# A hybrid decoder layer: 32x32 block transposes on VectorE, with the blocks placed by DMA, in place of TensorE transposes

## The chip, the cores and the metric

One Trainium2 chip, one core. Five engines run their own instruction streams: TensorE (PE; its weight loads are listed as PEld), VectorE (DVE), ScalarE (ACT), GpSimd (POOL) and SyncE (SP), which here only issues DMA transfers. Waits between them go over semaphores; an engine takes its instructions in order. The metric is device time in microseconds.

## The reference

One layer, float32, 1024 tokens of width 1024. One RMS norm feeds one input projection; its columns go to two groups that mix tokens side by side, whose outputs are joined, projected, added to x and followed by an RMS norm and an MLP of width 4096.

```python
# group A: differential attention, 4 heads of two 64-wide maps, values 128 wide
s = einsum(q, k) * scale;  p = softmax(causal(s))
a = p[:, :, 0] - lam * p[:, :, 1];  da_o = a @ v
da_o = rms_norm(da_o, da_out_norm_w) * (1 - lam_init)
# group B: gated delta rule, 4 heads of 128, q, k, v after a causal conv of width 4 and SiLU
S_t = a_t S_{t-1} (I - b_t k_t k_t^T) + b_t k_t v_t^T;   o_t = S_t^T q_t
dn_o = rms_norm(dn_o, dn_out_norm_w) * silu(z)
mix = concatenate([da_o, dn_o]);  x = x + mix @ w_out
x = x + square(relu(rms_norm(x, norm2_w) @ w_up)) @ w_down
```

## The kernel before, in words

A product in float32 precision is made of three products of rounded halves (`hH`, `hL` for activations, `wH`, `wL` for weights), so an activation is rounded by ACT into hH (a cast) and VectorE puts the rest into hL (a subtraction). hH and hL hold the operand with the channels on the partitions and the tokens along the free dimension; whoever makes rows of tokens must turn them. Until now TensorE does that, with `T.transpose` of 128x128 blocks against `ident`.

The stages around the change, in order of time:

- **Projections of the delta rule** (`dn_proj(kind)`, 0 for q, 1 for k, 2 for v; some 70 to 242 us). For each head h and half hf of the tokens PE makes 128 channels x 512 tokens (`trn`, lines 265 to 267), ACT and VectorE do the convolution (tile `cy`, L682) and SiLU. The result has channels on partitions. For the values, `transposed` (L716) turns four blocks on PE into PSUM (`ps_t`), VectorE multiplies by the factor vsc of each token (L854), and `park` (L702) stores the tile by SP into the DRAM array park_d, slot 2. `invert` and `horner` compute the inverse of the triangular matrix of each chunk of 128 tokens, W; horner reads 128-byte runs of fsg_d into `gb` (L804), turns them by `V.transpose` in 32x32 blocks (L806) and multiplies on PE. The order in this part is laid out by the tile framework's scheduler.
- **The interleaved part** (some 245 to 600 us). Generators with priorities yield to the class `Interleave`, a planner with estimated costs of ACT, VectorE and POOL (`act`, `vec`, `powr`), PE's pace, and holds on PSUM banks. It writes PE's order down at build time (`manual_schedule`); it has no cost for the SP or POOL queues' DMA issues, and gives a load from DRAM a fixed due time (`MIX_T`, 5 us). The other engines' orders come from the framework's scheduler.
  - `scan` runs the delta rule over 8 chunks: it loads `pka` (keys and values, L910), L918 to L947. `scan_out` makes the output rows: loads `pkb` and `zgt`, products L970 and L977, the norm's sums on ACT, its root on POOL (`rstd`, L291), a product with the gate per head into `oc` (L989), and a POOL-issued store to mixn_d (L991). `zgt` has one buffer.
  - `da_units` makes the projections of group A (L1067 to L1069; ps_qk is read out by ACT, L1078 to L1086), and fills PE between the others; `da_turns` turns its q and k on PE and stores them to qk_d from POOL (L1034).
  - `scores` and `values` do the attention, head 0, head 1, then heads 2 and 3 in turn. `load_head` reads keys (KS, L1118); `load_q` is four SP transfers (L1133, L1134) for one score, one score ahead. `values` turns the probabilities (L1238), multiplies (L1250, ps_o), and ACT copies and squares (L1259, L1260); VectorE writes the normed row (L1264). Heads 0 and 1 store theirs to mixa_d from POOL (L1266); for heads 2 and 3 the row stays in `mx`, beside which the first two heads' rows are loaded (L1231).
  - `mix_loads` loads rows of mixn_d into `mt` (L1295, two buffers) once the last projection unit has begun and the scan is done; `mixed` and `turn` (through `to_hT`, L298 to L304) turn a tile of mt or mx, four blocks on PE into a bank of the pool px, ACT casts to hH (L303), VectorE subtracts to hL (L304). `landed` tells `outproj` that a tile may be used. px has two banks, shared by da_turns, values and mixed.
  - `outproj` multiplies by w_out (L1340 to L1342) and fills PE in the later part.
- **The MLP** (from some 600 us) is not touched.

Of the kernel before, what the change touches and what calls it, by code (L numbers as in the profile page):

```python
# [120 lines left out]
def tile_hymba_layer(  # L121
# [537 lines left out]

    ssq, ssk, rq, bp, kds, vsc = smalls + [sp.tile([P, 32], F32, name=n) for n in ("kds", "vsc")]  # L660

    cps = [sa.tile([P, 1028], F32, name=f"cp{i}") for i in range(2)]
# [38 lines left out]
    def park(h, hf, slot, src):  # L701
        nc.sync.dma_start(park_d[h, 4 * hf:4 * hf + 4, :, slot, :].rearrange("c p d -> p c d"), v4(src))  # L702

    def cols4(t, h, hf):
# [92 lines left out]
    def horner(hs, hf):  # L797
# [16 lines left out]
        for m in (96, 64, 32):  # L814
            for h in hs:
# [7 lines left out]
                else:  # L823
                    S.activation(zv, pv4, AF.Copy, scale=-1.0)
        for h in hs:
            W[h, hf] = z[h]

    inverse = invert()
    for h, hf, q2 in skew(dn_proj(0)):
# [21 lines left out]
    for h, hf, v2 in skew(dn_proj(2)):  # L851
        ps = transposed(v2)
        vs = ta("kn", 2)
        V.tensor_tensor(v4(vs), v4(ps), bc_col(cols4(vsc, h, hf)), ALU.mult)  # L854
        park(h, hf, 2, vs)
        if hf == 0:
            horner(*heads.pop(0))
# [98 lines left out]
    def scan_out(c, Sold, yy):  # L956
# [31 lines left out]
        for h in range(HEADS):  # L988
            V.scalar_tensor_tensor(oc[:, h * P:(h + 1) * P], oc[:, h * P:(h + 1) * P], f[:, h:h + 1],  # L989
                                   zgt[:, h * P:(h + 1) * P], ALU.mult, ALU.mult)  # L990
        nc.gpsimd.dma_start(mixn_d[c], oc)  # L991
        flow.pe(4 * MM)
        t = flow.chain(vec(512))
        flow.hold("pB", t)
        flow.chain(*[act(P, True)] * 4, vec(4), powr(4), vec(4), *[vec(P, 60)] * 4, start=t)
        if c == NT - 1:
# [225 lines left out]
    def values():  # L1222
        for _ in order:
# [3 lines left out]
            if h == 2:  # L1227
                while "ax" not in pools or len(rows_of) + len([x for x in loads if not x[3]]) > 1:
                    yield flow.now + 50, None
                rows_of[tb] = pools["ax"].tile([P, 512], F32, tag="mx", name="mx", bufs=2)  # L1230
                nc.sync.dma_start(rows_of[tb][:, 0:256], mixa_d[tb])  # L1231
            ats = []
# [42 lines left out]
    tiles = list(reversed(range(NT)))  # L1275
    landed, hns = {}, {}

    def turn(r, src, t, tb, k0, keep=None):
# [8 lines left out]
    def mix_loads():  # L1287
        while not (pre and state["scan"]):
            yield flow.now + 200, None
        for i, t in enumerate(tiles):  # L1290
            while i >= 2 + state["mixed"]:
                yield flow.now + 50, None
            mt = pools["a2"].tile([P, 512], F32, tag="mt", name="mt", bufs=2)
            with tc.issue_after(newest["SP"].ins):
                nc.sync.dma_start(mt, mixn_d[t])  # L1295
            loads.append((mt, flow.now + MIX_T, t, 4))

    def mixed():
        for i in range(2 * NT):

            while not any(x[1] <= flow.now and x[2] in over for x in loads):
                yield flow.now + 50, None
            x = min((x for x in loads if x[2] in over), key=lambda x: x[1])
            r = yield from flow.bank("px")
            loads.remove(x)
            turn(r, *x)
            state["mixed"] += x[3] == 4
        while not state["attn"]:
# [609 lines left out]
```

## Time and profile before

| | |
|---|---|
| Median of three runs | 1234.93 us (1234.6 to 1235.82) |
| Profiled execution | 1234.74 us |
| Its span, first to last instruction | 1233.0 us |
| Busy: PE / PEld / DVE / ACT / POOL | 1217.3 / 1054.3 / 824.7 / 624.2 / 151.3 us |
| Granted TensorE clock | 1.00 |
| DMA | 143301 packets, 202.12 MB, mean 164 GB/s |

A row of a group reads: line, engine, operation, output tile <- input tiles, shapes, count, then busy time, the mean of one in ns, and the idle time before with what ended it. In a list in order of time the first two numbers are start and duration in us; "SPq" is an issue of a DMA by SP, and a bracket tells the idle time before and who ended it. A matmul's duration is longer than its step, since the next one starts before it has drained; the distance between two starts is what it costs. In the list of waits the numbers are total us, times, longest.

### The profile page before, as it was taken

To read this page: it belongs to the slowest core of one execution; us is meant where nothing else is said; L and a number is where in the kernel's file an instruction comes from. 1 tells how busy PE (TensorE), PEld (TensorE's weight loads), DVE (VectorE), ACT (ScalarE), POOL (GpSimd) and SP (SyncE) were. 2 spreads that over 40 slices of the span, in tenths; PEclk is the share of its full clock that TensorE was granted. 3 is DMA by queue.
4 is the path that set the end of the run, shared out by engine and by line. 5 is a ranking of instruction groups with operands and counts; after the bars stand their busy time and mean duration, and the time that the engine had idled before them with its cause. 6 is when DMAs were issued, how large, how long until landed. Compare 5 with 4: busy or idle time off the path is not lost.

```text
span 1233.0 us, 18819 instructions
## 1 busy us (share of the span) xinstructions
PE 1217.3 (99%) x6823; PEld 1054.3 (86%) x6823; DVE 824.7 (67%) x1524; ACT 624.2 (51%) x1249; POOL 151.3 (12%) x215
## 2 busy tenths in 40 slices
PE   9999999999999999999999999999999999999998
PEld 8978888898999998888888888888888888888886
DVE  6868796556647657777799544565569755777543
ACT  6588553344346555566666544444564333333330
POOL 2411110043434421001200000000000000000000
PEclk9999999999999999999999999999999999999999
DMA  9344653278748756323437434444479645423301
GB/s 350 98 115 122 163 162 104 63 234 240 231 148 252 232 162 159 85 77 108 157 117 255 172 122 151 171 170 153 155 241 382 234 179 184 163 103 103 137 35 69
DMA packets 143301, 202.12 MB, mean 164 GB/s; under 512 B 20920, under 2 KB 98280, under 8 KB 143208
## 3 DMA queue, kind: packets, MB, share of 16 engines
q1 hardware_dynamic: 138584, 187.28, 46.9%
q0 software_dynamic: 4480, 13.64, 2.9%
q8 instruction: 54, 0.88, 0.3%
q14 instruction: 39, 0.32, 0.1%
q10 hardware_dynamic: 144, 0.00, 0.0%
HBM read 135.86 MB, written 65.01 MB: 163 GB/s over the span
## 4 chain that ended last, share of the span: by engine, by line
PE 88%; DVE 4%; DMA 3%; ACT 2%; issue 2%; POOL 1%; SPq 1%; POOLq 0%; DVEq 0%; ACTq 0%
PE X L1517 4%; PE X L1515 4%; PE X L1516 4%; PE X L1814 4%; PE X L1815 4%; PE X L1813 4%; PE ps_dn L265 3%; PE ps_dn L267 3%; PE ps_dn L266 3%; PE ps_qk L1067 3%; PE ps_qk L1068 3%; PE ps_qk L1069 3%; PE ps_o L1250 2%; PE Y L1515 2%; PE Y L1517 2%; PE Y L1516 2%
## 5 line engine op out<-in xcount | busy, mean ns | idle before, releaser
L1433 ACT CAST hH<-ur 128x1024 fp32r<-128x1024 f32 x56 | 58.9, 1051 | 173.4 <-PE Y L1814 89.8
L1434 DVE TENSOR_TENSOR hL<-ur,hH 128x1024 fp32r<-128x1024 f32 x56 | 68.3, 1223 | 79.4 <-ACT hH L1433 79.4
L1067 PE MATMUL ps_qk<-wH,hH 128*128 128x256 f32 x384 | 114.3, 298 | 0.0
L1069 PE MATMUL ps_qk<-wH,hL 128*128 128x256 f32 x384 | 108.7, 283 | 0.0
L1068 PE MATMUL ps_qk<-wL,hH 128*128 128x256 f32 x384 | 108.4, 282 | 0.0
L1434 DVE TENSOR_TENSOR op<-raw,op 128x1024 fp32r<-128x1024 f32 x48 | 58.7, 1223 | 74.2 <-PE X L1516 41.1
L1813 PE MATMUL X<-hH 128*128 128x512 f32 x224 | 87.1, 389 | 0.0
L1814 PE MATMUL X<-hL,hH 128*128 128x512 f32 x224 | 87.1, 389 | 0.0
L1815 PE MATMUL X<-hH,hL 128*128 128x512 f32 x224 | 87.1, 389 | 0.0
L265 PE MATMUL ps_dn<-hH,wH 128*128 128x512 f32 x192 | 76.3, 397 | 0.2 <-ACT cp L678 0.2
L267 PE MATMUL ps_dn<-hH,wL 128*128 128x512 f32 x192 | 75.8, 396 | 0.0
L266 PE MATMUL ps_dn<-hL,wH 128*128 128x512 f32 x192 | 75.8, 395 | 0.0
L1068 PEld LDWEIGHTS ps_qk<-wL,hH 128*128 128x128 f32 x384 | 73.4, 191 | 0.2
L1067 PEld LDWEIGHTS ps_qk<-wH,hH 128*128 128x128 f32 x384 | 73.3, 191 | 0.2
L1069 PEld LDWEIGHTS ps_qk<-wH,hL 128*128 128x128 f32 x384 | 73.1, 190 | 0.0
L1434 DVE TENSOR_TENSOR hL<-dw,hH 128x1024 fp32r<-128x1024 f32 x56 | 68.2, 1218 | 0.9 <-ACT hH L1433 0.9
L1433 ACT CAST op<-raw 128x1024 fp32r<-128x1024 f32 x48 | 50.4, 1052 | 35.7 <-PE Y L1517 19.9
L1433 ACT CAST hH<-dw 128x1024 fp32r<-128x1024 f32 x56 | 58.7, 1048 | 10.7 <-DMA dw<-in_w_down_dram 5.0
L1205 ACT ACTIVATE pexp<-pexp,mx 128x128 f32<-128x128 f32 (+7 forms) x64 | 49.7, 777 | 25.1 <-DVE mx L1204 24.5
L682 DVE SCALAR_TENSOR_TENSOR cy<-cp,pv,cy 128x512 f32<-128x512 f32 x72 | 53.7, 747 | 8.1 <-ACT cy L680 7.3
L1340 PE MATMUL ps_op<-wH,hH 128*128 128x512 f32 x128 | 53.0, 414 | 0.0
L1515 PE MATMUL Y<-hH,op 128*128 128x512 f32 x128 | 49.9, 390 | 0.4 <-DVE ua L1555 0.4
(370 smaller groups left out, 3429.1 us busy)
## 6 DMA issues: line engine op xcount, KB each, us to landing
ur<-ud SPq DMA_DIRECT2D x28, 1024.0 KB, 5.0
raw<-in_w_up_dram SPq DMA_DIRECT2D x32, 512.0 KB, 3.9
dw<-in_w_down_dram SPq DMA_DIRECT2D x32, 512.0 KB, 6.8
wraw<-in_w_units_dram SPq DMA_DIRECT2D x48, 256.0 KB, 3.7
qk_d<-qa POOLq DMA_DIRECT2D x32, 256.0 KB, 4.3
ud<-ua SPq DMA_DIRECT2D x16, 512.0 KB, 4.2
ud<-s SPq DMA_DIRECT2D x16, 512.0 KB, 2.7
pka<-park_d SPq DMA_DIRECT2D x32, 192.0 KB, 4.8
```

Of the source, the lines that this page charges most:

```text
L265: T.matmul(ps, lh(k), rh(k), start=(k == 0), stop=False)
L266: T.matmul(ps, lh(k), rl(k), start=False, stop=False)
L267: T.matmul(ps, ll(k), rh(k), start=False, stop=(k == n - 1))
L1067: T.matmul(ps[:, :256], hH[:, k, sl], wh[:, k, :], start=(k == 0), stop=False)
L1068: T.matmul(ps[:, :256], hH[:, k, sl], wl[:, k, :], start=False, stop=False)
L1069: T.matmul(ps[:, :256], hL[:, k, sl], wh[:, k, :], start=False, stop=(k == KB - 1))
L1433: S.copy(dst[0], src)
L1434: V.tensor_tensor(dst[1], src, dst[0].bitcast(F32), ALU.subtract)
L1515: T.matmul(ps, op[0][:, k, cs], h[0][:, k, :], start=start and k == 0, stop=False, skip_group_check=True)
L1813: T.matmul(bank[t], v[0][:, j, sl], v[2][:, j], start=s0, stop=False, skip_group_check=True)
L1814: T.matmul(bank[t], v[0][:, j, sl], v[3][:, j], start=False, stop=False, skip_group_check=True)
L1815: T.matmul(bank[t], v[1][:, j, sl], v[2][:, j], start=False, stop=s1, skip_group_check=True)
```

## The change

Three sets of rows are turned differently. `V.transpose` turns each 32x32 block of a tile in place of the block; the blocks then still have to change places, and that is done by the addresses of DMA transfers with runs of 32 elements (128 bytes).

1. *Values of the delta rule.* VectorE block-transposes the tile (`vs`), and `put_blocks` stores it by four SP transfers into park_d instead of one. Since the tokens' factors vsc can no longer be applied on the way, W's rows are multiplied by them at the end of `horner`, and the factor of the other term, neg_eg, is divided by vsc.
2. *Outputs of the delta rule.* The gated product goes into zgt, `V.transpose` writes it to oc, and the store is as before. When it is read back, `get_blocks` uses four SP loads that put the blocks in place; `settle` casts and subtracts straight from mt, without PE and without a bank.
3. *Rows of heads 0 and 1.* The normed row is written to PSUM, transposed in blocks into om and stored; it comes back by `get_blocks` into the first half of mx. `turn_last` settles that half from the buffer and turns only the two blocks of heads 2 and 3 on PE.

The planner's entries follow: a 512-column transpose in scan_out, for heads 0 and 1 a hold of the bank up to the transpose, for heads 2 and 3 up to the end of the squares (before: up to the copy), two turned blocks instead of four, and none for mt.

```diff
+    rvs = ssk
...
+    def put_blocks(dst, src):
+
+        for a in range(4):
+            s = slice(32 * a, 32 * a + 32)
+            nc.sync.dma_start(dst[:, s].rearrange("(b s) r -> s b r", s=32),
+                              src[s].rearrange("s (b r) -> s b r", r=32))
+
+    def get_blocks(dst, src):
+
+        k = dst.shape[1] // P
+        src = src.rearrange("(a s) (k b r) -> b s k a r", s=32, k=k, r=32)
+        for b in range(4):
+            nc.sync.dma_start(dst[32 * b:32 * b + 32].rearrange("s (k a r) -> s k a r", k=k, r=32), src[b])
...
         for h in hs:
+            V.tensor_tensor(v4(z[h]), v4(z[h]), bc_col(cols4(vsc, h, hf)), ALU.mult)
             W[h, hf] = z[h]
 
+    V.reciprocal(rvs, vsc)
+    V.tensor_tensor(neg_eg, neg_eg, rvs, ALU.mult)
     inverse = invert()
...
     for h, hf, v2 in skew(dn_proj(2)):
-        ps = transposed(v2)
         vs = ta("kn", 2)
-        V.tensor_tensor(v4(vs), v4(ps), bc_col(cols4(vsc, h, hf)), ALU.mult)
-        park(h, hf, 2, vs)
+        V.transpose(vs, v2)
+        put_blocks(park_d[h, 4 * hf:4 * hf + 4, :, 2, :].rearrange("c p d -> (c p) d"), vs)
...
         for h in range(HEADS):
-            V.scalar_tensor_tensor(oc[:, h * P:(h + 1) * P], oc[:, h * P:(h + 1) * P], f[:, h:h + 1],
-                                   zgt[:, h * P:(h + 1) * P], ALU.mult, ALU.mult)
+            hs = slice(h * P, (h + 1) * P)
+            V.scalar_tensor_tensor(zgt[:, hs], oc[:, hs], f[:, h:h + 1], zgt[:, hs], ALU.mult, ALU.mult)
+        V.transpose(oc, zgt)
         nc.gpsimd.dma_start(mixn_d[c], oc)
...
-                nc.sync.dma_start(rows_of[tb][:, 0:256], mixa_d[tb])
+                get_blocks(rows_of[tb][:, 0:256], mixa_d[tb])
...
-            V.scalar_tensor_tensor(om, om, f, dawb, ALU.mult, ALU.mult)
-            if h < 2:
-                nc.gpsimd.dma_start(mixa_d[tb, :, h * P:(h + 1) * P], om)
             flow.pe((tb + 1) * MM)
             t = flow.chain(act(P))
+            if h < 2:
+                V.scalar_tensor_tensor(po[:, 2 * P:3 * P], om, f, dawb, ALU.mult, ALU.mult)
+                V.transpose(om, po[:, 2 * P:3 * P])
+                nc.gpsimd.dma_start(mixa_d[tb, :, h * P:(h + 1) * P], om)
+                flow.hold(r, flow.chain(act(P, True), vec(1), powr(1), vec(1), vec(P, 60), vec(P, 60), start=t))
+                continue
+            V.scalar_tensor_tensor(om, om, f, dawb, ALU.mult, ALU.mult)
+            t = flow.chain(act(P, True), start=t)
             flow.hold(r, t)
-            t = flow.chain(act(P, True), vec(1), powr(1), vec(1), vec(P, 60), start=t)
+            t = flow.chain(vec(1), powr(1), vec(1), vec(P, 60), start=t)
...
+    def settle(src, tb, ks, t=None):
+        sl = slice(tb * P, (tb + 1) * P)
+        sv = src.rearrange("p (k t) -> p k t", t=P)
+        S.copy(hH[:, ks, sl], sv)
+        V.tensor_tensor(hL[:, ks, sl], sv, hH[:, ks, sl].bitcast(F32), ALU.subtract)
+        n = P * (ks.stop - ks.start)
+        return flow.chain(act(n), vec(n), start=t)
+
+    def turn_last(r, src, t, tb):
+        settle(src[:, 0:256], tb, slice(0, 2))
+        ps = bank_tile(px, r, "ps_tr")
+        for j in (2, 3):
+            T.transpose(ps[:, j * P:(j + 1) * P], src[:, j * P:(j + 1) * P], ident)
+        flow.pe(2 * TR)
+        t = settle(ps[:, 256:512], tb, slice(2, 4))
+        flow.hold(r, t)
+        landed[tb, 0] = t
...
-                nc.sync.dma_start(mt, mixn_d[t])
+                get_blocks(mt, mixn_d[t])
...
+            if x[3] == 4:
+                loads.remove(x)
+                landed[x[2], 4] = settle(x[0], x[2], slice(4, 8))
+                state["mixed"] += 1
+                continue
             r = yield from flow.bank("px")
             loads.remove(x)
-            turn(r, *x)
-            state["mixed"] += x[3] == 4
+            turn_last(r, *x[:3])
```

More of the change, by code (lines that the diff above doesn't have):

```diff
@@ L994, in scan_out @@
         flow.hold("pB", t)
-        flow.chain(*[act(P, True)] * 4, vec(4), powr(4), vec(4), *[vec(P, 60)] * 4, start=t)
+        flow.chain(*[act(P, True)] * 4, vec(4), powr(4), vec(4), *[vec(P, 60)] * 4, vec(512, 100), start=t)
         if c == NT - 1:
```

## The prediction

> **What bounds the kernel now.** I read the page's first part, then the waits of TensorE (PE), the stages' busy times, and for each edited step its own rows in order of time.
>
> ```profile
> span 1233.0 us, 18819 instructions
> PE 1217.3 (99%) x6823; PEld 1054.3 (86%) x6823; DVE 824.7 (67%) x1524; ACT 624.2 (51%) x1249; POOL 151.3 (12%) x215
> ...
> PE ps_qkt L1028 <- ACT ps_o L1260: 1.1, 2, 0.8
> PE ps_at L1238 <- ACT ps_o L1260: 0.8, 2, 0.7
> ...
> 210.00:240.00 30.00, 30.00 (x233) 26.35 (x231) 17.18 (x27) 11.11 (x24) 0.00 (x0) 1.00 0.28 79
> 270.00:300.00 30.00, 27.75 (x236) 27.26 (x235) 19.37 (x61) 11.43 (x35) 11.92 (x15) 1.00 0.81 240
> 420.00:450.00 30.00, 29.83 (x254) 29.63 (x253) 16.70 (x52) 16.29 (x46) 10.87 (x17) 1.00 0.71 201
> 540.00:570.00 30.00, 28.96 (x176) 25.18 (x177) 23.28 (x83) 20.40 (x64) 3.84 (x7) 1.00 0.37 104
> ```
>
> PE has work in 1217.3 of 1233.0 us, and of its waits I show the two that the change touches. The stage rows (length, then PE, weight loads, DVE, ACT, POOL, clock, DMA share, GB/s) show full or nearly full PE wherever the change acts, with DVE and ACT well below. So time is the sum of PE's work plus the short holes, and an instruction taken from PE is worth its issue interval, provided nothing new makes PE wait: its order is written out beforehand, and it does not step past a late operand.
>
> **What is removed from PE.** A transpose's duration in the groups (0.27 us) overlaps the next, so I take intervals.
>
> ```profile
> 431.30 0.60 PE L298 MATMUL ps_tr<-ident,mt 128*128 128x128 f32 x4
> 431.74 0.27 PE L1028 MATMUL ps_qkt<-ident,qn 128*128 128x128 f32 x1
> ...
> L716 PE MATMUL ps_t<-ident,cth x32: 270/272/329, 141.9 to 240.9; 128*128 128x128 f32 x32
> L298 PE MATMUL ps_tr<-ident,mx x32: 270/272/273, 517.4 to 582.5; 128*128 128x128 f32 x32
> ```
>
> Four transposes hold PE from 431.30 to 431.74, 0.11 us each. Those on the values' tiles (L716) and on mx have the same form and the same single duration, so I price them alike. The change removes 32 for the delta rule's values (8 half-heads x 4), the 32 on mt, and half of the 32 on mx: 80 x 0.11 = **8.8 us**. The ends of this term are close together.
>
> **Values (dn_proj(2)).** VectorE's product L854 from PSUM becomes a block transpose of the same size; eight scalings of W and two 32-column operations come on top.
>
> ```profile
> L806 DVE STREAM_TRANSPOSE W<-gb 128x512 f32<-128x512 f32 x8 | 5.6, 703 | 1.5 <-DMA gb<-fsg_d 1.4
> L854 DVE TENSOR_TENSOR kn<-ps_t,vsc 128x512 f32<-128x512 f32 x8 | 5.4, 678 | 2.6 <-PE ps_t L716 2.6
> ...
> 242.67 0.38 SPq L702 DMA_DIRECT2D park_d<-kn  x1
> 249.42 1.76 SPq L910 DMA_DIRECT2D pka<-park_d  x4
> ...
> L1118 SPq DMA_DIRECT2D KS<-qk_d x16: 605/633/1028, 289.6 to 481.2; - x16
> ```
>
> Exchange: 0.703 - 0.678, nothing. Scalings: 8 x 0.68 = 5.4 us of VectorE, beside a PE that is full while VectorE works 17 of 30 us; if that cover went, only the last pair (1.4 us) would stand ahead of the first projection units. The reciprocal and the product on 32 columns come where VectorE waits for the inverse's load anyway: 0. Each store of 512 runs becomes four of 512 shorter ones. A KS load too is 512 runs and costs SP 0.633 us, so a half-head costs 4 x 0.633 - 0.38 = 2.15 us more of SP, 17 us over some 52. What queues behind are horner's gb loads, weight loads, and at the end the pka loads that start the scan: the last store's four issues end near 242.67 + 2.5 = 245.2, and the pka loads came at 249.42, so about 4 us stand against a landing. I take +0.5 us for late gb loads (nearest row: PE is full from 210 to 240 although gb loads share SP's queue); ends 0 and +2.5, one full set of four issues.
>
> **Outputs (scan_out).** A 0.70 us transpose stands between the four products of L989 and the store to mixn_d. That store heads POOL's queue, which is the one place where I see it reach PE:
>
> ```profile
> 285.47 0.60 POOL L991 DMA_DIRECT2D mixn_d<-oc  x1 [1.67 <-DVE oc L989]
> 286.07 0.54 POOL L1034 DMA_DIRECT2D qk_d<-qa  x1
> ...
> 286.07 3.48 DMA qk_d<-qa
> 292.43 6.03 DMA pkb<-park_d
> 298.51 1.18 PE ps_o L970 x6
> ```
>
> In the chain that ended last POOL waits for oc, the qk_d store stands behind, SP waits for its landing, then KS and pkb loads follow, and PE is out of work near 298. Here 0.7 us arrive nearly whole: +0.6; ends 0 (POOL elsewhere stands idle most of the time) and +1.3. The buffer zgt is held 0.7 us longer, and SP's next zgt load with it; included in that upper end. The other seven transposes lie beside PE work. For the two early heads a product now goes to PSUM and a 128-column transpose follows: 16 x some 0.3 us on a VectorE with 10 us free in 30, ahead of the mixa_d stores: 0, the same upper end.
>
> **PSUM holds.** The planner now keeps a ps_o bank until the squares are done (all heads), or the transpose (early heads). The waits on L1260 above, 1.1 + 0.8 us, came because it was planned free too soon: -1.0, between 0 and -1.9; a longer hold costs PE nothing while projection units fill in.
>
> **Loads of mixn_d.** One load of 128 rows becomes four of 512 runs of 128 bytes; ACT and VectorE cut straight from the buffer.
>
> ```profile
> mt<-mixn_d SPq DMA_DIRECT2D x8, 256.0 KB, 3.4
> 431.93 0.33 SPq L1295 DMA_DIRECT2D mt<-mixn_d  x1
> 431.94 0.59 ACT L303 CAST hH<-ps_tr 128x512 fp32r<-128x512 f32 x1 [1.40 <-PE ps_tr L298]
> 460.27 0.59 ACT L303 CAST hH<-ps_tr 128x512 fp32r<-128x512 f32 x1
> 439.97 0.69 DVE L304 TENSOR_TENSOR hL<-ps_tr,hH 128x512 fp32r<-128x512 f32 x1 [0.76 <-ACT hH L303]
> ...
> q1 hardware_dynamic: 138584, 187.28, 46.9%
> q1 hardware_dynamic: 1285, 0.15, 24.5%
> gb<-fsg_d SPq DMA_DIRECT2D x9, 16.0 KB, 1.8
> ```
>
> The second q1 row is of 196 to 200 us, where only gb loads (128-byte runs) move: 0.245 x 16 x 4 us / 1285 = 12.2 ns a packet; the whole program has 0.469 x 16 x 1233 / 138584 = 66.8 ns for 1351 bytes. A tile's 2048 runs are then 1.56 us of all sixteen engines against 0.81 before. At share 0.71 that fits. The tile loaded at 431.93 met VectorE's part at 439.97; ACT's cast of 0.59 comes right before, so load to cast was 7.4 us. The buffer is now free only after VectorE's part, two parts or 1.3 us later, which leaves 6.1. Needed: three more issues, 1.9, and the landing of 3.4: 5.3. So 0, with 0.8 us to spare; the other end is rival three.
>
> **Loads of mixa_d.** The same with four of 256 runs, but here SP is short of time:
>
> ```profile
> 543.88 0.33 SPq L1231 DMA_DIRECT2D mx<-mixa_d  x1
> 546.74 0.59 SPq L1134 DMA_DIRECT2D qb<-qk_d  x1
> 549.86 0.42 PE L1193 MATMUL ps_sc<-KS,qa 128*128 128x384 f32 x1
> 555.79 0.33 SPq L1231 DMA_DIRECT2D mx<-mixa_d  x1
> 558.01 0.59 SPq L1134 DMA_DIRECT2D qb<-qk_d  x1
> 560.38 0.28 PE L1193 MATMUL ps_sc<-KS,qa 128*128 128x256 f32 x1
> 566.15 0.33 SPq L1231 DMA_DIRECT2D mx<-mixa_d  x1
> 566.54 0.45 SPq L1134 DMA_DIRECT2D qb<-qk_d  x1
> 568.75 0.33 PE L1194 MATMUL ps_sc<-KS,qb 128*128 128x128 f32 x1
> ...
> DMA to landing us min/median/max: 2.1/2.2/2.5
> ```
>
> Behind an mx load stand the four q loads of a coming score; the last row is their landing in 500 to 580 us. 546.74 + 2.2 leaves 0.9 us before the product at 549.86; 558.01 + 2.2 leaves 0.2; 566.54 + 2.2 nothing (568.75). Three more issues of 0.59 are 1.8 us each time: 0.9 + 1.6 + 1.8 = 4.3 us of new PE waits if all three meet. The plan moves, so not every mx load will fall just ahead of such q loads: I take two of three, +3.0; ends 0 and 4.3. Cutting a tile in two halves (settle twice) adds one ACT and one VectorE part per tile; the first half needs no transpose and can go early, the second is shorter than before: 0.
>
> By the Trainium skill, page "DMA: Bandwidth & Descriptors", section "Issuing engines are not separate DMA queues", the time that a queue takes to start a transfer is usually small beside the transfer; by that this term would be nothing and the sum 1226. The trace disagrees at this place: four starts take as long as the landing.
>
> **Sum.** -8.8 + 0.5 + 0.6 - 1.0 + 3.0 = -5.7 us on the profiled execution's 1234.74 (its span 1233.0 and 1.7 around it), which is 0.2 below the median 1234.93: **1229.0**.
>
> **Rivals.** *One, the saving arrives whole*: SP finds room for every added start. For it: three places out of eight mx loads are all that I find. Against: exactly these. -8.8 = **1226**.
>
> *Two, the new waits eat it*: every term at its upper end, 4.3 + 1.3 + 2.5 and no gain from the holds, 8.1 of 8.8: **1234**, no change. For it: the reordered plan could fall into as many holes as the present one (2.25 us in 270 to 300); against: each upper end is one coincidence.
>
> *Three, short runs land late, and it gets slower.* Place: 417 to 460 us, the cast of a mixn_d tile on ACT, in order ahead of ps_qk read-outs; PE fills its two banks and stops. It bites from a landing of 6.1 - 1.9 = 4.2 us on. If landing grew with the number of runs, four times gb's 1.8 us for 128 runs, it is 7.2; a buffer then turns in 1.9 + 7.2 + 1.3 = 10.4 us, two buffers give a tile per 5.2 us against 4.05 now (seven from 431.94 to 460.27), 8 x 1.15 = 9.2 us: 1229.0 + 9.2 = **1238**. From a landing of 6.3 us on, my 5.7 us are gone (4.05 + 5.7 / 8 = 4.76 a tile). Against: the gb loads' fixed part is paid once a load, not once a run, and packets of 12.2 ns leave room.
>
> The Trainium skill, page "VectorE: DVE Perf Modes", section "The three transpose paths", warns that a plain copy that transposes by its access pattern is 19 times slower than the dedicated path. Taken literally on 0.81 us of data time a tile, an estimate of 15 us a tile and over 80 us in all; the gb loads' packets speak against it, since here whole 128-byte runs move and not single elements, so it adds nothing to this rival's chance.
>
> **Chances.** Forecast 0.40 (1226.5 to 1232), rival one 0.25, two 0.17, three 0.18. Faster by over 0.2% (2.5 us, about what a measurement of this kernel tells from no change): 0.66, within: 0.16, slower: 0.18. The range goes from rival one with part of the hold's gain, 1224.5, to rival three with the mx term at its end, 1239.5, and leaves out some 0.15.
>
> **What would show it.** PE has 6743 matmuls and some 8.8 us less busy time; rows on mt vanish from the transposes and mx has 16. Right: new PE waits on q loads (DMA qa or qb) of 2 to 4 us in all between 530 and 575 us, none on mixn_d tiles, landing of mt under 4.2 us, fewer waits on the squares of L1260. Wrong: landings of mt above 6 us, ACT waiting for DMA mt, PE waits in the values' stage, or holes in the reordered plan that no step here names.

## The result and the profile after

The changed kernel takes 1237.78 us (median, 1236.36 to 1239.42); the kernel before took 1235.53 us (1234.24 to 1238.19) beside it. The ratio is 1.0016, 95% interval 1.0009 to 1.0024: slower by 0.16%, where 1229.0 had been forecast. By the bound of 0.2% it is no change, by its interval a small loss. The 80 transposes are gone, and no gain came of it.

The profiled execution took 1237.01 us. The first part of its page, and then its busy times by stage (length, then PE, weight loads, DVE, ACT, POOL with their counts, granted clock, DMA share, GB/s):

```profile
span 1235.3 us, 18817 instructions
PE 1215.0 (98%) x6743; PEld 1047.7 (85%) x6743; DVE 838.3 (68%) x1566; ACT 624.5 (51%) x1257; POOL 151.6 (12%) x215
```

```profile
245.00:455.00 210.00, 204.17 (x1701) 199.52 (x1701) 137.66 (x412) 108.38 (x310) 83.80 (x114) 1.00 0.72 218
455.00:485.00 30.00, 28.21 (x152) 23.48 (x153) 23.26 (x57) 18.03 (x42) 4.56 (x8) 1.00 0.58 159
485.00:585.00 100.00, 99.32 (x585) 85.42 (x584) 73.03 (x209) 62.39 (x178) 13.87 (x23) 1.00 0.33 90
585.00:612.00 27.00, 25.32 (x130) 20.66 (x128) 18.71 (x41) 17.20 (x42) 5.87 (x8) 1.00 0.50 176
612.00:624.00 12.00, 10.05 (x41) 7.86 (x42) 10.55 (x20) 8.10 (x16) 1.64 (x2) 0.72 0.54 165
```

The same view of the kernel before, at the two stages that differ most:

```profile
455.00:485.00 30.00, 30.00 (x180) 26.58 (x179) 23.53 (x56) 18.91 (x44) 5.61 (x10) 1.00 0.54 144
612.00:624.00 12.00, 12.00 (x69) 10.15 (x68) 10.26 (x21) 8.62 (x19) 1.69 (x3) 1.00 0.77 242
```

PE issues 6743 products, 80 fewer, and yet its busy time fell by 2.3 us only. Two things stand in the table. Between 455 and 485 PE has holes that were not there. Between 612 and 624 it idles, and its granted clock is 0.72: 12 x 0.28 = 3.4 us of PE's time are lost to the clock alone, inside the busy time.

Summed from start to start, the transposes on mt and mx went from 6.3 to 1.4 us and those of the delta rule's part from 9.9 to 6.9: 7.9 us saved, 0.10 each. The last ps_dn product (the projections of the delta rule) starts 3.9 us earlier, but some products of horner have moved behind it; the last of those starts 2.4 us earlier. Up to the first ps_op product PE does the same work as before, less 64 transposes and four scores, 6.7 us in all; it starts 4.3 us earlier, so some 2 us of the saving were gone by 456 us. The last ps_op product starts only 0.1 us earlier, and the first product X of the MLP 2.3 us later. PE's waits between its instructions rose from 9.7 to 14.3 us. The list of PE's waits between 245 and 640 us, before and then after (us in total, times, longest; dots stand for rows left out), says for what:

```profile
PE ps_qkt L1028 <- DVE qn L1092: 1.3, 2, 1.0
PE ps_o L970 <- DMA pkb<-park_d: 1.2, 1, 1.2
...
PE ps_sc L1194 <- DMA qb<-qk_d: 0.5, 1, 0.5
...
```

```profile
PE ps_qkt L1046 <- DVE qn L1110: 4.1, 5, 1.1
PE ps_tr L1491 <- DVE nrt L290: 3.0, 1, 3.0
PE ps_sc L1212 <- DMA qb<-qk_d: 0.9, 1, 0.9
PE ps_sc L1211 <- DMA qa<-qk_d: 0.7, 1, 0.7
...
PE ps_sc L1211 <- issue: 0.6, 1, 0.6
PE ps_at L1256 <- ACT ps_o L1278: 0.4, 1, 0.4
PE ps_o L987 <- DMA pkb<-park_d: 0.4, 1, 0.4
...
```

```profile
613.28 0.30 PE L1491 MATMUL ps_tr<-ident,hn 128*128 128x128 f32 x1 [2.96 <-DVE nrt L290]
```

New are: more waits on q and k rows (qn) that VectorE finishes late, waits on q loads, and one wait of 2.96 us near 613, the largest, with the low clock behind it. The profile puts that one down to "DVE nrt", the semaphore that came last; the experiments show what it was.

### The profile page after: what moved, and what is told of

Same layout as the page of the kernel before. It is cut to its first block, busy times and chain, and to the rows that moved or that the text cites. A ratio compares the mean times of both kernels' runs of the same rounds, so it can differ in the third digit from the quotient of the medians.

```text
span 1235.3 us, 18817 instructions
## 1 busy us (share of the span) xinstructions
PE 1215.0 (98%) x6743; PEld 1047.7 (85%) x6743; DVE 838.3 (68%) x1566; ACT 624.5 (51%) x1257; POOL 151.6 (12%) x215
## 4 chain that ended last, share of the span: by engine, by line
PE 88%; DMA 4%; DVE 3%; ACT 2%; SPq 1%; issue 1%; POOL 0%; DVEq 0%; ACTq 0%
PE X L1561 5%; PE X L1560 5%; PE X L1562 5%; PE X L1860 4%; PE X L1858 4%; PE X L1859 4%; PE ps_dn L265 3%; PE ps_dn L267 3%; PE ps_dn L266 3%; PE ps_qk L1085 3%; PE ps_qk L1086 3%; PE ps_qk L1087 3%; PE Y L1561 2%; PE Y L1560 2%; PE Y L1562 2%; PE ps_o L1268 2%
## 5 line engine op out<-in xcount | busy, mean ns | idle before, releaser
L1387 PE MATMUL ps_op<-wH,hL 128*128 128x512 f32 x128 | 50.4, 394 | 0.0
```

## The experiments

All ratios are to the kernel before, run beside the experiment. Three theories stood at the start: *ACT behind mx* (casts of mx that wait for their loads in ACT's queue hold up the attention), *SP at 410 to 480* (32 issues for mt delay the q loads), and *re-planning* (PE's written order falls into new holes wherever it is shifted). A fourth, *holds*, came after the first four.

**Each part alone.** The first is the change of the values only, the second that of the outputs only, the third that of heads 0 and 1, the fourth all but the third. No line is new in them; each takes its hunks of the change's diff. Against the kernel before, the core of e_values, e_outputs and e_heads01 in turn; e_no_heads01 is the first two together, with the holds as before:

```diff
-        park(h, hf, 2, vs)
+        V.transpose(vs, v2)
+        put_blocks(park_d[h, 4 * hf:4 * hf + 4, :, 2, :].rearrange("c p d -> (c p) d"), vs)
```

```diff
+        V.transpose(oc, zgt)
...
-                nc.sync.dma_start(mt, mixn_d[t])
+                get_blocks(mt, mixn_d[t])
...
+                landed[x[2], 4] = settle(x[0], x[2], slice(4, 8))
```

```diff
-                nc.sync.dma_start(rows_of[tb][:, 0:256], mixa_d[tb])
+                get_blocks(rows_of[tb][:, 0:256], mixa_d[tb])
...
+                V.scalar_tensor_tensor(po[:, 2 * P:3 * P], om, f, dawb, ALU.mult, ALU.mult)
+                V.transpose(om, po[:, 2 * P:3 * P])
...
+            turn_last(r, *x[:3])
```

> Only the values of the delta rule are turned in blocks (put_blocks, vsc in W, neg_eg divided); outputs and the rows of heads 0 and 1 as before. All theories agree on the saving of 32 transposes, 3.5 us; in the changed kernel the end of the last projection ps_dn came 3.9 us earlier. Theory 'parts' (the loss is made by the later parts): 1231 to 1232 us, faster by 3 to 4 us, and no holes of PE over 2 us near 610 us. Theory 're-planning' (any shift of the later plan can lose what was won): anywhere from 1231 to 1236.

> Only the delta rule's outputs are turned in blocks (transpose in scan_out, four loads per tile of mt, settle from mt); values and rows of heads 0 and 1 as before. Saving on PE 32 x 0.10 = 3.3 us. Theory 'ACT behind mx' (the mixa part made the loss): 1232 us. Theory 'SP at 410 to 480' (the 32 mt issues of 0.64 us that split the q loads made it): 1234 to 1237, with PE waits on the q loads (qa, qb) of 1 us or more together between 440 and 490.

> Only the rows of heads 0 and 1 are turned in blocks (transpose after the norm, four loads per half of mx, turn_last), with the holds of the changed kernel; values and outputs as before. Saving on PE 16 x 0.10 = 1.6 us. Theory 'ACT behind mx': slower, 1237 to 1240, with ACT waiting 4 us or more for mx loads between 500 and 580. Theory 'SP at 410 to 480': 1233 to 1235. My recorded prediction for this part alone: -1.8 - 1.0 + 3.0, so 1235.

> The changed kernel with the rows of heads 0 and 1 (and the holds) as before: values and outputs in blocks. Theory 'ACT behind mx': 64 transposes x 0.10 = -6.5 us arrive nearly whole, 1229 us, and the late hole of 3 us near 613 with the half clock behind it is gone. Theory 'SP at 410 to 480': 1234 to 1236. If it loses as much as the changed kernel, the rows of heads 0 and 1 aren't the cause.

Measured: 0.9993 (0.9985 to 1.0002), 1.0032 (1.002 to 1.0043), 1.0104 (1.0091 to 1.0118), 1.0027 (1.0018 to 1.0036). Every part saves its transposes, and three of the four kernels are slower than before. The parts don't add up either (differences of the medians): -0.9, +3.8 and +12.7 us alone, and +2.3 for all three. Leaving out heads 0 and 1 does not bring the time back, so *ACT behind mx* isn't what made the loss. With the values alone, PE's timeline shows one new long wait and, by stage, the clock behind it:

```profile
297.83 0.58 PE L987 MATMUL ps_o<-S,pkb 128*128 128x128 f32 x1 [2.56 <-DMA pkb<-park_d]
```

```profile
296.00:300.00 4.00, 2.17 (x10) 2.17 (x11) 0.77 (x3) 0.00 (x0) 0.29 (x1) 0.73 0.97 328
300.00:304.00 4.00, 4.00 (x30) 3.83 (x30) 2.91 (x10) 1.85 (x5) 0.60 (x1) 0.84 0.62 181
```

2.56 us of waiting, against 1.21 at this place before, and 4 x (0.27 + 0.16) = 1.7 us lost to the clock: 3.1 of the 3.0 to 3.5 us that the values save. The profiled execution is the slowest of the eleven; those without the low clock lose less. With the outputs alone the wait is on a q load behind mt loads, as *SP at 410 to 480* has it:

```profile
461.74 0.39 PE L1208 MATMUL ps_sc<-KS,qa 128*128 128x320 f32 x1 [3.13 <-DMA qa<-qk_d]
```

With heads 0 and 1 alone there are six waits of 1.2 to 2.6 us, the largest on a product of VectorE for the probabilities at 597 (2.56), two more on the bank that is now held up to V.transpose (1.94 and 1.23), two on the turns behind the norms (2.05 and 2.00). *Re-planning* had said no more than that it would be somewhere; it needed a mechanism per place.

**The holds.** In PE's written order 99 ps_op products stand behind the last ps_o, where 138 stood before. Theory *holds* took the planner's longer holds of ps_o for the cause, and the missing 39 products for the cover that is lacking at 613.

Against the changed kernel, e_old_holds_23; e_old_holds does the same for heads 0 and 1 too:

```diff
-            t = flow.chain(act(P, True), start=t)
             flow.hold(r, t)
-            t = flow.chain(vec(1), powr(1), vec(1), vec(P, 60), start=t)
+            t = flow.chain(act(P, True), vec(1), powr(1), vec(1), vec(P, 60), start=t)
```

e_squares_hold makes the opposite edit in the kernel before, for all heads. e_row_in_sbuf against the changed kernel:

```diff
-                V.scalar_tensor_tensor(po[:, 2 * P:3 * P], om, f, dawb, ALU.mult, ALU.mult)
-                V.transpose(om, po[:, 2 * P:3 * P])
-                nc.gpsimd.dma_start(mixa_d[tb, :, h * P:(h + 1) * P], om)
-                flow.hold(r, flow.chain(act(P, True), vec(1), powr(1), vec(1), vec(P, 60), vec(P, 60), start=t))
+                V.scalar_tensor_tensor(om, om, f, dawb, ALU.mult, ALU.mult)
+                ot = ap.tile([P, P], F32, tag="ot", name="ot", bufs=1)
+                V.transpose(ot, om)
+                nc.gpsimd.dma_start(mixa_d[tb, :, h * P:(h + 1) * P], ot)
+                flow.hold(r, flow.chain(act(P, True), start=t))
```

> The changed kernel, but the planner frees a ps_o bank after ACT's copy for all heads, as before the change; nothing else. In the plan this leaves 150 ps_op products behind the last ps_o in place of 99 (138 before the change). Theory 'holds' (the longer planned holds push attention back in PE's order, so that too little out-projection work is left to cover the norms and turns at its end): the wait of 2.96 us at 613 and the half clock behind it go, 5 to 6 us, and new waits of PE on banks that are in truth still read (squares, transposes of heads 0 and 1) cost 2 to 4: 1233 to 1235. Theory 're-planning by chance': the hole at the end stays or shows up elsewhere, 1236 to 1239. By the term of my prediction (longer holds save 1.0 us): slower, 1239.

> The changed kernel, but for heads 2 and 3 the planner frees the ps_o bank after the copy as before; heads 0 and 1 keep the hold up to the transpose. In the plan 123 ps_op products stand behind the last ps_o in place of 99. It undoes the term that my prediction put at -1.0 us. By that term: slower by 1 us, 1239. By theory 'holds': the late attention is paid at the end, so with 123 the wait and the half clock near 613 shrink, waits on squares of some 1.5 us come back: 1233 to 1236.

> The kernel before, with one change: the planner keeps a ps_o bank until the squares are done, for all heads. No transpose is saved. In the plan 99 ps_op products stand behind the last ps_o in place of 138, as in the changed kernel. By the term of my prediction: -1.0 us, 1234. By theory 'holds': the wait on squares (1.9 us) goes, but a wait of 2 us or more opens between 600 and 640: 1236 to 1239.

> The changed kernel, but for heads 0 and 1 the normed row stays in SBUF (om) and is block-transposed into another SBUF tile (ot), so that the ps_o bank is free after the squares, and the planner's hold ends there. In the plan 135 ps_op products stand behind the last ps_o in place of 99. Theory 'holds': no wait over 1 us near 613, no half clock there, and no new bank waits: 1231 to 1233, and so the first kernel here faster than before. Theory 're-planning by chance': 1236 to 1239.

Measured: 1.0265 (1.025 to 1.028), 1.0054 (1.0042 to 1.0066), 1.0029 (1.0017 to 1.004), 1.0061 (1.0047 to 1.0075). Three of the four miss what *holds* expected; the fourth, e_squares_hold, has the time that it expected and its wait at another place. With the old holds for heads 0 and 1 the planner frees banks that VectorE still reads (PE's waits, 245 to 600 us):

```profile
PE ps_at L1256 <- DVE om L1286: 13.7, 8, 3.2
PE ps_qkt L1046 <- DVE om L1286: 7.4, 3, 2.6
```

So that hold was needed. With the row in SBUF (e_row_in_sbuf) there is little waiting at the end, 0.8 us, but 3.11 and 2.15 us on scores at 462.7 and 490.5. The hold up to the squares, added to the kernel before, does not remove the waits on the squares: there are two in place of four, but of 4.3 us in all in place of 1.9. At the longer one ACT gets to the squares later than the planner thinks; by the profile its copy into om, just ahead of them, waits 2.29 us for an earlier store of om to mixa_d to land.

```profile
387.29 0.33 PE L1042 MATMUL ps_qkt<-ident,qn 128*128 128x128 f32 x1 [3.23 <-ACT ps_o L1274]
```

There PE has no wait between 585 and 624, although 99 products are left as in the changed kernel: the count of products is not the cause at 613. And taking this hold away from heads 2 and 3 of the changed kernel costs time (from 1.0016 to 1.0054), as adding it to the kernel before does: its sign depends on the rest of the order. In e_old_holds_23 the wait that my prediction had placed on the q loads behind mx does appear:

```profile
573.22 0.30 PE L1211 MATMUL ps_sc<-KS,qa 128*128 128x128 f32 x1 [1.72 <-DMA qa<-qk_d]
582.53 0.38 PE L1268 MATMUL ps_o<-vt,at 128*128 128x128 f32 x1 [2.08 <-ACT ps_o L1278]
```

**Another queue for the blocks.** The mt loads by POOL; the placing by the stores, which leaves one load per tile of mt, with the stores on SP or on POOL (both on top of the values and of the later keys, below).

First e_mt_by_pool (get_blocks issues on the queue that it is given), then e_outputs_put; e_outputs_put_pool has nc.gpsimd in place of nc.sync in the latter:

```diff
-                get_blocks(mt, mixn_d[t])
+                get_blocks(mt, mixn_d[t], nc.gpsimd)
```

```diff
-        nc.gpsimd.dma_start(mixn_d[c], oc)
+        dst = mixn_d[c].rearrange("(b s) (k a r) -> a s k b r", s=32, k=4, r=32)
+        for a in range(4):
+            nc.sync.dma_start(dst[a], oc[32 * a:32 * a + 32].rearrange("s (k b r) -> s k b r", k=4, r=32))
...
-                get_blocks(mt, mixn_d[t])
+                nc.sync.dma_start(mt, mixn_d[t])
```

> The changed kernel, but the 32 loads of mt are issued by POOL and not by SP; PE's order is identical. Theory 'SP at 410 to 480': the waits of PE on the q loads at 455, 464 and 480 (0.87 + 0.61 + 0.68 us) go, and 1.5 to 2.2 us come if nothing takes their place: 1236. Theory 'moved': POOL's stores and roots stand behind loads that wait for a buffer, and new waits on them eat it: 1237 to 1239.

> The kernel with the values and the later keys, plus the outputs in blocks, but placed by the stores: SP stores oc by four transfers, and mt is loaded by one transfer as before; rows of heads 0 and 1 as before. Theory 'SP at 410 to 480' (four loads a tile in front of the q loads cost what the transposes save): without them the second saving of 3.1 us arrives, no wait of 2.5 us on q loads at 460: 1227.5 to 1229. Rival 're-planning by chance': a wait of the same size turns up elsewhere (stores that wait for oc in SP's queue ahead of pkb, or q loads again): 1231 to 1235.

> As e_outputs_put (values in blocks, later keys, outputs placed by the stores, mt by one load), but the 32 stores are issued by POOL. Theory 'a queue takes it where nothing waits': POOL's roots and stores stand behind four issues of some 0.6 us a chunk; if that is covered, the second saving of 3.1 us arrives: 1227 to 1229. Theory 'it moves': waits on rnt (a root on POOL) of 1.5 to 3 us, or on the first scores, 1231 to 1235.

Measured: 1.0122 (1.0106 to 1.0138), 1.0019 (1.0007 to 1.0031), 1.0042 (1.0029 to 1.0055). The waits on q loads between 455 and 480 go in all three, and something else stands behind the four issues each time. POOL's queue with the mt loads, and the wait on a root (rnt) that POOL works out behind them:

```profile
365.37 5.87 POOL L717 DMA_DIRECT2D mt<-mixn_d  x8 [1.43 <-PE ps_at L1256]
```

```profile
373.99 0.30 PE L1046 MATMUL ps_qkt<-ident,qn 128*128 128x128 f32 x1 [3.10 <-DVE rnt L290]
```

SP's queue with the stores, between two halves of the first scores' q loads (PE waits 3.57 us at 362.70):

```profile
358.42 0.53 SPq L1153 DMA_DIRECT2D qa<-qk_d  x1
359.05 2.77 SPq L1011 DMA_DIRECT2D mixn_d<-oc  x4
362.49 0.48 SPq L1154 DMA_DIRECT2D qb<-qk_d  x1
```

With the stores on POOL, four of them hold its queue for 3.00 us from 302.03 on, ahead of a root, and PE waits 1.69 and 2.04 us for qn at 307.34 and 310.53.

So the price of placing blocks is a queue's time, some 2.6 us and more for the four transfers of a tile, and here none of the three places had that time free.

**The wait at 297.** Head 0's key loads (KS), not needed before 362 us, wait at the head of SP's queue for a store, with the pkb loads behind. Only SP's order is changed; PE's stays as it is.

```diff
-        heads[0] = load_head(0, ap), load_v(0, ap)
-        q = load_q(*order[0])
...
+        with tc.issue_after(newest["pkb"].ins): heads[0], q = (load_head(0, ap), load_v(0, ap)), load_q(*order[0])
```

> Only the values in blocks, and the loads of head 0's keys (KS, needed from some 362 us) are ordered behind the next pkb loads in SP's queue instead of ahead of them; PE's order is identical to that with the values alone. That one had a wait of 2.56 us on pkb at 298 and, in six of eleven executions, a stretch of half clock. Theory 'one hole and its clock': the wait falls below 0.5 us and no execution shows a clock under 0.999: 1230.5 to 1232, faster than before by 3 to 4.5 us, so the whole saving of the values. Rival 'moved': KS and the first q loads land later and the wait shows up on the first scores at 362: 1233 to 1235.

> The kernel before, with head 0's key loads behind the next pkb loads; nothing in blocks, PE's order identical to before. The wait of 1.21 us on pkb goes: 1233 to 1234. If the values' saving of 3.0 to 3.5 us in e_values_keys_later was whole, this one is 3 to 4 us slower than that: 1233 to 1234 as well. If it reaches 1231 or less, the order of the loads made most of that gain.

Measured: 1229.83 us, 0.9959 (0.9947 to 0.9971), and 0.9983 (0.9974 to 0.9992). In both profiles the wait on pkb is gone, a wait of 1.0 us on qn stands near its place (297.29 and 300.58), and no clock below 1.00 follows. By the medians the order of the loads alone is worth 0.17%, some 2 us; its profiled execution, with 9.8 us of PE's waits in all where the kernel before has 9.7, does not show where they come from. The values are worth another 0.24%, some 3 us, as much as their 32 transposes. e_values_keys_later is the fastest kernel here:

```profile
span 1227.7 us, 18798 instructions
PE 1213.2 (99%) x6791; PEld 1050.3 (86%) x6791; DVE 829.8 (68%) x1534; ACT 624.8 (51%) x1249; POOL 151.4 (12%) x215
```

**The wait at 613.** First the plan there is spread, then the one operand that seems late is moved with PE's order unchanged.

In turn e_turns_spread, e_casts_later (casts() holds the splits of first_ops(0) back that have not been written down) and, on top of that, e_casts_and_settles:

```diff
-        flow.hold(r, t)
+        flow.hold(r, t + (0.0 if keep is None else 2500.0))
```

```diff
-                split((o[:, 0, :, cs], o[:, 1, :, cs]), raw)
+                todo_casts.append((o[:, 0, :, cs], o[:, 1, :, cs], raw))
+            if g or tag == "wH": casts()
...
+                if d == 3:
+                    with tc.issue_after(newest["kept"].ins): casts()
```

```diff
-        S.copy(hH[:, ks, sl], sv)
+        with tc.issue_after(newest["ACT"].ins): S.copy(hH[:, ks, sl], sv)
```

> The changed kernel, but the planner keeps the banks of the first four norm rows' turns 2.5 us longer, which spreads these turns over the out-projection's last products; PE's order is the same as in the changed kernel up to some 595 us. It prices the wait at 613 and what follows it. Theory 'one hole and its clock': if the wait of 2.96 us goes, so does the stretch of 6.8 us at half clock, and both together are worth 5 to 6 us: 1232 to 1233. If the clock fell for another reason, the half clock stays and 3 us come: 1235. Theory 'the chain at the end is long' (norm, turn, cast, in a row, are short of cover however spread): the wait only moves, 1236 to 1239.

> The changed kernel; two casts of the first up-projection weights (wL<-wraw), which waited for their load on ACT ahead of the copies that free PE's banks at 611, stand behind those copies. PE's order is identical. Theory 'a late operand': the copies come some 2.3 us earlier, the wait of 2.96 us at 613 shrinks to under 1, and without the long wait there is no half clock: 3 + 3 us, 1231.5 to 1233. Theory 'it moves': the products or turns behind wait for the casts or for the norms instead, and the total stays within 1.5 us of the changed kernel, 1236 to 1239.

> As e_casts_later, and the casts of settle stand behind the copies of probabilities that were planned before them, so that ACT does not wait for mx loads (5.8 us in six waits before). PE's order is identical. PE had almost no wait between 490 and 583 in the changed kernel, so theory 'PE's waits alone count': the same time as e_casts_later within 1 us. Theory 'ACT behind mx': 2 us or more faster than that.

Measured: 1.0029 (1.0017 to 1.004), 1.0032 (1.0019 to 1.0045), 1.0004 (0.9995 to 1.0013). Spread, the wait breaks into four of 0.7 to 1.7 us with a clock of 0.89 and 0.68 in 616 to 624. With the casts out of the way it stays, 3.16 us at 616.48. Ordering settle's casts as well gives some 0.3% against e_casts_later in the medians, so ACT's waits for mx count for something after all; the two profiled executions took the same time (1238.3 and 1238.5 us), so they don't show where it came from, and that stays open. The wait near 614 remains (3.28). The chain of work that ended last shows why the casts were the wrong operand. In the changed kernel, and then in e_casts_later (start, length, what):

```profile
605.79 0.61 DVE acc L1392
606.42 4.84 DMA acc_d<-acc
611.33 0.59 ACT kept L302
```

```profile
608.79 0.61 DVE acc L1392
609.42 4.90 DMA acc_d<-acc
...
614.40 0.59 ACT kept L302
```

The copies into `kept` free the two banks that PE waits for, and in both kernels they start 0.07 to 0.08 us after a store of `acc` has landed. `kept`, `raw` and `acc` are tiles of one set of eight row buffers. In the changed kernel the raw loads of the MLP's weights come ahead of the fourth kept row and have taken the next two buffers to come free, so it gets one whose store is issued only at 606.42. In the kernel before, that row's copies (607.90, 610.40) came ahead of the first raw load. SP's queue, after, then before:

```profile
596.82 0.38 SPq L1538 DMA_DIRECT2D raw<-in_w_up_dram  x1
599.36 0.32 SPq L1403 DMA_DIRECT2D acc_d<-acc  x1
604.65 0.38 SPq L1538 DMA_DIRECT2D raw<-in_w_up_dram  x1
...
606.42 2.96 SPq L1403 DMA_DIRECT2D acc_d<-acc  x2
```

```profile
611.40 0.37 SPq L1493 DMA_DIRECT2D raw<-in_w_up_dram  x1
```

e_kept_row_first lets the fourth kept row take its buffer first (kept4 is set once that row's copies are written down) and orders the raw loads behind the copies; e_all_orders adds the later keys and the settles. All three parts of the change and PE's order are kept.

```diff
-        while len(kept) == 4 and len(raws) < 4 and 4 + len(raws) in normed2:
+        while "kept4" in state and len(raws) < 4 and 4 + len(raws) in normed2:
...
+                if d == 3:
+                    state["kept4"] = True
...
-                feed()
+                with tc.issue_after(newest["kept"].ins): feed()
```

> As e_casts_later, and the loads of the later up-projection weights (raw) take their row buffers only after the fourth kept row has taken its own, so that this row gets the buffer whose store was issued one place earlier on SP (three places earlier in the list) instead of the one of 606.42. PE's order is identical. Theory 'the row buffer': the copies into kept follow the transposes at once, the wait near 613 to 616 falls from 3 us to under 1, and with it goes the half clock: 1232 to 1235. Rival 'the chain of norms is long': the wait only shrinks to 2 us or moves to the next turns, 1236 to 1239.

> e_kept_row_first, with the casts of settle behind the copies of probabilities and head 0's key loads behind the next pkb loads: all repairs of order together, all three parts of the change kept, PE's order as in the changed kernel. If each repair gives what it gave alone or should give (settles 1 to 3, keys 1 to 2, row 3 to 5): 1229 to 1233, faster than before. If a new wait takes over: 1234 to 1238.

Measured: 1233.93 us, 0.9989 (0.998 to 0.9998), and 1232.14 us, 0.9974 (0.9963 to 0.9984). Against e_casts_later it is 0.4% for the order in which one buffer is taken. The fourth row's copies in e_kept_row_first follow their transposes and no longer a store, and the stage of the end:

```profile
606.82 0.59 ACT L302 COPY kept<-ps_tr 128x512 f32<-128x512 f32 x1 [1.38 <-PE ps_tr L298]
```

```profile
612.00:624.00 12.00, 9.33 (x54) 7.33 (x52) 9.52 (x20) 8.84 (x19) 1.41 (x2) 1.00 0.67 231
```

The clock stays at 1.00, and 54 products stand where the changed kernel had 41. Waits of PE remain on the turns behind (0.7, 0.7 and 1.3 us, 2.7 between 585 and 624 where the changed kernel had 3.6), so the rival had that part right. Over the whole profiled execution PE waits 15.6 us, not less than the changed kernel's 14.3; what the repair gives, 0.27% against the changed kernel, is the size of the 3.4 us that the clock had cost. The mean clock was 0.996 to 0.998 in all twelve executions of the changed kernel and 0.998 to 1.000 in the eleven of e_kept_row_first. So the wait of 2.96 us and the half clock behind it came of the fourth kept row's buffer.

With it the changed kernel is 0.11% faster than before, and with the other repairs of order 0.26%. But one of these repairs, the later keys, gives the kernel before 0.17% too. Against that kernel some 0.09% is left, about 1 us, and the two intervals overlap: of the 7.9 us that three parts save, no more is shown to be kept with all repairs, and it is still slower than the values alone with the later keys. Why the raw rows came first in the changed order was not tested.

## Why the prediction was wrong

- *80 transposes, -8.8.* Right in kind, 7.9 measured, 0.10 us each and not 0.11.
- *Values, +0.5.* The size was near, 1.1, and the place was another. PE shows no new wait up to 245 us, so the gb loads were not late; but from start to start the products of horner (ps_p and ps_h) take 1.1 us more in every kernel here with the values in blocks, and in none without. Why is not shown.
- *Outputs, +0.6 by way of the store at the head of POOL's queue.* The wrong place. On POOL the qk_d store went ahead of the mixn_d store, and the wait on pkb fell from 1.2 to 0.4. Instead the waits on qn rose from 1.3 to 4.1 us. One of 1.1 us near 322 stands in every kernel here with the outputs in blocks and in none without. No block transpose lies on VectorE from 311.5 to 326 us there; VectorE idles 1.18 us for ps_A and then has three of four updates of S ahead of qn. So it is the order around the transposes that is another, and not 0.7 us in the way; what moved it was not tested.
- *PSUM holds, -1.0.* In the changed kernel the waits on the squares went from 1.9 to 0.4, but "a longer hold costs PE nothing while projection units fill in" was wrong: the hold alone makes the kernel before 0.29% slower, some 3.6 us, with 4.3 us of waits on the squares.
- *Loads of mixn_d, 0.* The landing was 3.3 us (median) and up to 4.7, above the 4.2 that I had set as the point from which it bites; no wait of PE came from the landing itself. What did reach PE was the queue: eight issues stood between the two halves of a q load.

```profile
444.92 0.49 SPq L1151 DMA_DIRECT2D qa<-qk_d  x1
445.51 6.32 SPq L717 DMA_DIRECT2D mt<-mixn_d  x8
451.87 0.62 SPq L217 DMA_DIRECT2D wraw<-in_w_halves_dram  x1
452.54 0.48 SPq L1152 DMA_DIRECT2D qb<-qk_d  x1
```

```profile
455.50 0.41 PE L1212 MATMUL ps_sc<-KS,qb 128*128 128x320 f32 x1 [0.87 <-DMA qb<-qk_d]
```

  0.9 us in the changed kernel, and 3.13 with the outputs alone, by the very mechanism that I priced for mx and left out for mt, where each tile has twice the runs. The two later waits on q loads (0.61 us at 464.46, 0.68 at 479.57) come more than 12 us behind the last of these issues; that they stem from them is not shown.
- *Loads of mixa_d, +3.0 at 543 to 569.* Not there: 0.4 us of PE waits in 485 to 585. The plan had moved, as I feared, but as a whole. In e_old_holds_23 the wait is there.
- *By the Trainium skill this term would be nothing* ("DMA: Bandwidth & Descriptors", section "Issuing engines are not separate DMA queues"). It came out near nothing, but not for the page's reason: the four issues of an mx load still took 2.56 us, longer than their landing of 2.2, and the eight for mt 6.32. They only stood where no product waited for the loads behind.
- *In no term:* the wait of 2.96 us and the clock, 3.4 us, together 6.4 of the some 10 us between the saving and the result. All new waits together are 4.6 us. The last 2 us lie in longer steps of PE's products from start to start: the 1.1 of horner, and small amounts over the others, of which the cause stays open. The prediction's last sentence names "holes in the reordered plan that no step here names" as a way to be wrong. It gave them no price, and rival two, "the new waits eat it" (1234, 0.17), came to the nearest time by other steps; that is luck.

The step that failed is the sum itself: waits were priced only where the change's own instructions stand, in an order taken over from before, and the clock was not priced at all. The order was rewritten from 245 us on, and the two largest new waits, 2.96 us near 613 and 1.12 near 322, belong to tiles that the change does not touch. What bears this out is that with PE's order left as it is, and only a late operand put right, time came back: the values' whole saving in e_values_keys_later, 0.27% in e_kept_row_first, 0.42% in e_all_orders, of which 0.17% is the keys' that the kernel before can have too.

## What to carry to other kernels

Where PE is full and its order is written out by a planner, an instruction saved is worth its time only after the new order has been searched for waits: look for the one or two longest, follow each in the chain of waits past the engine that the page names to the transfer or buffer behind it, and repair that without touching the order. A transfer split in four costs its queue the time of four issues (2.6 us on SP and 2.9 to 3.0 on POOL for a tile of mt or oc here), and the one to check is the load that stands behind it. Tiles that share a rotating set of buffers get them in the order in which they are written down, so a prefetch that is moved ahead can take the buffer of a row that is needed sooner.

## What was not expected of the hardware

PE's clock can halve behind a wait of 2 to 3 us. The changed kernel by stage, behind the wait of 2.96 us:

```profile
612.00:616.00 4.00, 2.42 (x11) 1.59 (x11) 3.33 (x7) 3.33 (x7) 0.55 (x1) 0.81 0.45 132
616.00:620.00 4.00, 3.63 (x11) 3.05 (x12) 3.22 (x8) 3.07 (x7) 1.08 (x1) 0.50 0.78 260
620.00:624.00 4.00, 4.00 (x21) 3.22 (x20) 4.00 (x8) 1.70 (x3) 0.00 (x0) 0.84 0.39 103
```

4 x (0.19 + 0.50 + 0.16) = 3.4 us lost, so 6.8 us at half clock. Behind 2.56 us in e_values, and behind 2.08 us in e_old_holds_23, it is 1.7 us lost, 3.4 at half clock. In e_turns_spread it is 1.7 us too, behind four waits within 6 us of which the longest is 1.67. But behind 3.13 us in e_outputs (461.74) nothing:

```profile
460.00:464.00 4.00, 2.27 (x13) 2.12 (x14) 2.66 (x5) 0.99 (x2) 0.25 (x1) 1.00 0.66 190
464.00:468.00 4.00, 4.00 (x26) 3.48 (x25) 2.05 (x6) 1.80 (x6) 0.00 (x0) 1.00 0.89 248
```

nor behind 3.23 us in the profiled execution of e_squares_hold. It is a matter of chance for one kernel, too: of the eleven executions of e_values five had a mean clock of 1.000 and took 1233.4 us (median), six had 0.997 or 0.998 and took 1235.1. The Trainium skill, page "TensorE: Matmul & The Clock Gate", section "Part 1: The HAM clock gate (the "warmup" mystery)", gives a free-running window of about 3.4 us after which an idle PE falls to half clock. The stretches of 3.4 and 6.8 us agree with one and two such windows, and a window that runs free would explain the chance; that one wait of 2.1 us can be enough is a measurement of these runs and less than the page's figure. The traces' records of the granted clock bear the window out: between the first and the last change of a trace each half-clock stretch lasts 3.41 or 6.83 us, and the full-clock stretches between two changes are whole multiples of 3.413 us (604.16 us is 177 of them, 17.07 is 5). With the clock, a wait of 2 to 3 us cost up to some twice its length, and so the repairs that removed such a wait were worth more than the wait (e_values_keys_later against e_values) or gave back the clock alone (e_kept_row_first against the changed kernel).
